# Which engine subtracts the low parts of an input projection's weights: GpSimd or VectorE

## The chip, the cores and the metric

The kernel runs on one core of a Trainium2 chip. The core has five engines that each work through a row of instructions of their own, in order: TensorE (PE: matrix products and transposes), VectorE (DVE), ScalarE (ACT), GpSimd (POOL) and SyncE (SP, which issues the DMAs). An instruction starts when the one ahead of it on its engine is through and the semaphores that it waits for are set. The metric is the time of one execution on the device, in microseconds (us).

## The reference

One layer of a hybrid block over a sequence of S = 1024 rows of D = 1024 numbers, all float32:

```python
u = rms_norm(h, norm_gain)
proj = u @ w_in                      # -> z_ssd, xbc, dt_raw, q, k, v, z_attn
xbc = silu(causal_depthwise_conv(xbc, conv_w, conv_b))        # 4 taps
dt = softplus(dt_raw + dt_bias);  a = -exp(a_log)
y = ssd_chunked(xs, dt, a, B, C) + xs * d_skip                # chunks of 128 rows
y_ssd = gated_group_rms_norm(y, z_ssd, ssd_norm_gain)
attn = diff_attention(q, k, v, lam, slopes)   # two softmaxes a head, one minus lam times the other
y_attn = rms_norm(attn, subln_gain) * (1 - lambda_init) * silu(z_attn)
h = h + concat([y_ssd, y_attn]) @ w_out
out = rms_norm(h, final_norm_gain)
```

## The kernel before

The two big projections are made on PE in a split form. Each operand is held as a high part, rounded to the type fp32r, and a low part, which is the operand minus the high part; a product is then three matmuls: high by high, high by low and low by high. For the input, `uh` and `ul` are made once at the start (L188 and L189, in two halves of 512 rows). The weights come in blocks of 128 columns: SP's queue loads `raw` (two buffers), ACT rounds it to `hi` (L199), and the low part `lo` is `raw - hi` (L200). `load_w` does this for two blocks at a time, into two buffers each of `hi` and `lo` (the tags whi and wlo). It is called 25 times: for B and C (bc, names of tiles lo_bc0 and so on), the conv inputs (xs), the gate of the SSD part (z), the queries and keys of a head (qk), the values of two heads (v) and their gate (za). The very first block (z0 with dt) isn't made by `load_w` but by a loop of its own, L333 to L343, with its subtraction on GpSimd at L342.

The program's stages are: the normalization of x (square sums on ACT, L173 and L175 the reciprocal root on GpSimd, L183 the scaling on DVE, L187 eight rounds of transposes on PE); the first block (L352 to L357, eight tiles of 128 rows, in two PSUM banks named mm); two groups g of the SSD part; and eight attention heads, whose projections are woven among the heads' own work, and the output projection. In a group, L281 and L282 (ACT) take a conv input from PSUM, L287 (DVE) adds three taps, L291 (ACT) is the tanh, L292 (DVE) finishes it; L374 and L376 make the masked product of B and C, L432 transposes, L457 and L463 are the group's other work on GpSimd. In attention, L557 makes a block of scores (PE), L563 adds the distance and takes the row maximum (DVE), L573 scales it, L581 is the exponential (ACT), L590, L591 and L594 weigh the two maps (DVE), L602 transposes them (PE), L605 copies them (ACT), and L609 multiplies by the values (PE). L507 and L508 take the queries out of their mm bank, L518 and L519 the keys; the bank is free for PE's next projection (L208 to L210 by columns, L217 to L219 by rows) after the DVE one of the two. L614 takes an attention output from PSUM. Some low parts of the output projection's weights are subtracted on GpSimd (L694, first half) and some on DVE (L694, second half, named wp_lo).

The order in which each engine gets its instructions isn't the order of the code: a scheduler arranges them by a simulated timeline of all engines, so that a change of one instruction's engine also moves others.

Of the kernel before, what the change touches and what calls it, by code (L numbers as in the profile page):

```python
# [8 lines left out]
F32 = mybir.dt.float32  # L9
# [3 lines left out]
ALU = mybir.AluOpType  # L13
# [25 lines left out]
def kernel(  # L39
# [11 lines left out]
    V, A, G, T = nc.vector, nc.scalar, nc.gpsimd, nc.tensor  # L51
# [8 lines left out]
    def big_tile(tag, bufs, shape, dt=F32, name=None):  # L60
        return big.tile(shape, dt, tag=tag, bufs=bufs, name=name or tag)
# [7 lines left out]
    def tG(shape, dt=F32, name="tG"):  # L69
        return big_tile("G", 13, shape, dt, name)  # L70
# [47 lines left out]
    def load_raw(blocks, name):  # L118
        raws = []
        for n, b in enumerate(blocks):  # L120
            raw = tRaw(f"raw_{name}{n}")
            dma(raw, w_blocks[b])
            raws.append(raw)
        return raws
# [69 lines left out]
    def load_w(b0, b1, name, raws=None):  # L194
        hi = big_tile("whi", 2, [P, ND, 2 * P], F32R, f"hi_{name}")
        lo = big_tile("wlo", 2, [P, ND, 2 * P], F32R, f"lo_{name}")
        for n, raw in enumerate(raws or load_raw((b0, b1), name)):
            cut = slice(n * P, (n + 1) * P)
            A.activation(hi[:, :, cut], raw, AF.Copy)  # L199
            G.tensor_tensor(lo[:, :, cut], raw, hi[:, :, cut].bitcast(F32), ALU.subtract)  # L200
        return hi, lo

    def proj_ch(w, n, half, ps):
# [130 lines left out]
    for d0, d1 in D3:  # L334
        hi, lo = (tG([P, d1 - d0, NZ], F32R, f"wz_{n}{d0}") for n in ("hi", "lo"))
        for n, raw in enumerate(raw_z0 + [wdt_raw]):
            cut = slice(n * P, min(NZ, (n + 1) * P))
# [22 lines left out]
    def ssd_group(g):  # L360
        hs = slice(8 * g, 8 * g + 8)
        w = load_w(B_XBC + 8 + g, B_XBC + 10 + g, f"bc{g}", raw_bc0 if g == 0 else None)
        if g == 0:
            bT, cT = conv_first(w)
# [18 lines left out]
        for k in range(2):  # L383
            w = load_w(B_XBC + 4 * g + 2 * k, B_XBC + 4 * g + 2 * k + 1, f"xs{g}{k}")
            for n in range(2):
                xsT.append(conv(w, n, 4 * g + 2 * k + n))
        if g == 0:
            z0 = z_first
        else:
            zw = load_w(B_Z + 4 * g, B_Z + 4 * g + 1, f"z{g}0")  # L390
            z0 = [proj_gate_half(zw, half, f"z{g}0{half}") for half in range(2)]
# [475 lines left out]
```

## Time and profile before

| | us |
|---|---|
| median of 3 runs | 1061.67 (1061.25 to 1062.02) |
| the profiled execution | 1060.02 |
| its span, first to last instruction | 1058.3 |
| PE busy | 1026.2 |
| DVE busy | 579.2 |
| ACT busy | 504.9 |
| POOL busy | 237.1 |

In the rows of the profile, L12 is line 12 of the program. A row of a timeline gives the start, the duration, the engine, the line, the operation, what is written and read with its shape, how many instructions are joined in the row, and in brackets how long the engine was idle ahead of it and what it waited for. A row of a group gives the total, the mean in ns and, behind the second bar, the idle time ahead of the group's instructions. A row of PE's waits gives the waiting and the awaited instruction, the total in us, the number of times and the longest. A row of a window gives the stretch, its length, the busy time and count of PE, of its weight loads (PEld), DVE, ACT and POOL, and then the clock granted to PE (1 is full), the share of DMA and GB/s. In a timeline the ends of an instruction and the start of the next overlap by some hundredths.

### The profile page before, as it was taken

The page shows a single profiled execution, that of the slowest core. Times are in us where ns is not written, and L with a number is a line of the kernel's source. Part 1 is how long each engine was busy: PE and PEld are TensorE (multiplying, and loading weights), DVE is VectorE, ACT ScalarE, POOL GpSimd, SP SyncE. Part 2 cuts the span into 40 slices and gives each one's busy share as a digit, 9 for nine tenths or more (in the row PEclk, how much of TensorE's full clock was granted, in tenths as well). Part 3 has the DMA queues.
Part 4 walks back from the last instruction along what each step waited for, and adds up shares of the span by engine and source line. Part 5 has one row for each costly group of instructions (what it writes and reads, how often), then busy time and mean ns, then how long its engine had stood idle before and what let it go on. Part 6 is the DMA issues. An engine that isn't in the chain of part 4 may idle for free.

```text
span 1058.3 us, 16243 instructions
## 1 busy us (share of the span) xinstructions
PE 1026.2 (97%) x6334; PEld 910.3 (86%) x6334; DVE 579.2 (55%) x1235; ACT 504.9 (48%) x1137; POOL 237.1 (22%) x191
## 2 busy tenths in 40 slices
PE   5999999989999999999999999999999998999997
PEld 5988887878987999889998899988998987788887
DVE  5546578665567264473563744627547587462221
ACT  8244367834456554453453554534646556341110
POOL 7212226422343312210222022111220340010000
PEclk9999999999999999999999999999999999999999
DMA  7111124221224311312103221033211533354211
GB/s 288 41 62 41 60 71 130 80 60 60 81 62 138 101 41 41 80 40 71 41 15 95 61 61 61 11 80 80 62 55 31 155 115 127 135 158 140 80 45 40
DMA packets 52085, 84.54 MB, mean 80 GB/s; under 512 B 3932, under 2 KB 30633, under 8 KB 52009
## 3 DMA queue, kind: packets, MB, share of 16 engines
q1 hardware_dynamic: 52008, 83.51, 25.5%
q8 instruction: 50, 0.82, 0.3%
q14 instruction: 27, 0.21, 0.1%
HBM read 62.45 MB, written 12.65 MB: 71 GB/s over the span
## 4 chain that ended last, share of the span: by engine, by line
PE 88%; DVE 5%; ACT 3%; DMA 2%; issue 2%; SPq 0%; POOLq 0%; DVEq 0%; ACTq 0%
PE mm L208 9%; PE mm L209 9%; PE mm L210 9%; PE mm L217 8%; PE mm L218 8%; PE mm L219 8%; PE o L609 6%; PE S L557 5%; PE mm L709 5%; PE mm L710 5%; PE mm L711 5%; PE tp L602 3%; PE S L439 3%; PE S L448 1%; PE S L452 1%
## 5 line engine op out<-in xcount | busy, mean ns | idle before, releaser
L563 DVE CUSTOM_DVE_ANT_0 s<-S,dist 128x256 f32<-128x256 f32 (+7 forms) x128 | 95.1, 754 | 99.8 <-PE S L557 94.5
L581 ACT ACTIVATE s<-s,small 128x256 f32<-128x256 f32 (+7 forms) x128 | 98.8, 772 | 89.4 <-DVE small L573 88.5
L208 PE MATMUL mm<-uh,hi_qk 128*128 128x512 f32 x256 | 101.4, 396 | 0.3 <-DVE k L519 0.3
L210 PE MATMUL mm<-uh,lo_qk 128*128 128x512 f32 x256 | 101.5, 396 | 0.0
L209 PE MATMUL mm<-ul,hi_qk 128*128 128x512 f32 x256 | 100.7, 393 | 0.0
L557 PE MATMUL S<-k,q 128*128 128x512 f32 (+2 forms) x384 | 92.8, 356 | 2.3 <-DVE small L563 2.3
L605 ACT ACTIVATE wT<-tp 128x512 f32<-128x512 f32 (+2 forms) x96 | 46.5, 485 | 82.9 <-PE tp L602 82.4
L609 PE MATMUL o<-v,wT 128*128 128x128 f32 x576 | 80.3, 276 | 0.0
L609 PEld LDWEIGHTS o<-v,wT 128*128 128x128 f32 x576 | 75.1, 193 | 2.4
L557 PEld LDWEIGHTS S<-k,q 128*128 128x128 f32 x384 | 65.1, 189 | 12.4 <-DVE small L563 4.2
L287 DVE SCALAR_TENSOR_TENSOR ca<-cr,cwb,ca 128x1023 f32<-128x1023 f32 (+2 forms) x36 | 56.8, 1578 | 33.3 <-ACT ca L282 32.5
L217 PE MATMUL mm<-hi_v,uh 128*128 128x256 f32 x256 | 73.6, 288 | 1.1 <-DVE q L508 0.9
L219 PE MATMUL mm<-hi_v,ul 128*128 128x256 f32 x256 | 73.4, 287 | 0.0
L218 PE MATMUL mm<-lo_v,uh 128*128 128x256 f32 x256 | 73.4, 287 | 0.0
L219 PE MATMUL mm<-hi_za,ul 128*128 128x256 f32 x256 | 73.0, 285 | 0.0
L217 PE MATMUL mm<-hi_za,uh 128*128 128x256 f32 x256 | 73.0, 285 | 0.0
L218 PE MATMUL mm<-lo_za,uh 128*128 128x256 f32 x256 | 73.0, 285 | 0.0
L200 POOL TENSOR_TENSOR lo_qk<-raw_qk,hi_qk 128x1024 fp32r<-128x1024 f32 x16 | 38.5, 2427 | 127.8 <-ACT hi_qk L199 127.8
L217 PE MATMUL mm<-hi_z,uh 128*128 128x256 f32 x192 | 56.1, 292 | 0.3 <-DVE z L322 0.3
L210 PEld LDWEIGHTS mm<-uh,lo_qk 128*128 128x128 f32 x256 | 48.1, 188 | 9.5 <-issue 0.2
L208 PEld LDWEIGHTS mm<-uh,hi_qk 128*128 128x128 f32 x256 | 48.2, 188 | 9.1 <-DVE k L519 0.6
L209 PEld LDWEIGHTS mm<-ul,hi_qk 128*128 128x128 f32 x256 | 48.2, 188 | 9.0
(217 smaller groups left out, 2762.7 us busy)
## 6 DMA issues: line engine op xcount, KB each, us to landing
m<-acs_d SPq DMA_DIRECT2D x16, 512.0 KB, 3.8
raw_qk<-in_w_blocks_dram SPq DMA_DIRECT2D x16, 512.0 KB, 3.6
q<-q SPq DMA_DIRECT2D x32, 256.0 KB, 3.0
rwo<-in_w_out_dram SPq DMA_DIRECT2D x16, 512.0 KB, 3.5
rt<-tt_d SPq DMA_DIRECT2D x27, 256.0 KB, 3.7
x<-in_x_dram SPq DMA_DIRECT2D x8, 512.0 KB, 6.2
raw_z<-in_w_blocks_dram SPq DMA_DIRECT2D x8, 512.0 KB, 3.5
raw_xs<-in_w_blocks_dram SPq DMA_DIRECT2D x8, 512.0 KB, 3.7
```

What stands on the lines that cost most here:

```text
L208: T.matmul(ps, hi[:, d, cut], uh[half][:, d, :], start=(d == 0), stop=False)
L209: T.matmul(ps, hi[:, d, cut], ul[half][:, d, :], start=False, stop=False)
L210: T.matmul(ps, lo[:, d, cut], uh[half][:, d, :], start=False, stop=(d == ND - 1))
L217: T.matmul(ps, uh[half][:, d, cut], hi[:, d, :], start=(d == 0), stop=False)
L218: T.matmul(ps, uh[half][:, d, cut], lo[:, d, :], start=False, stop=False)
L219: T.matmul(ps, ul[half][:, d, cut], hi[:, d, :], start=False, stop=(d == ND - 1))
L287: V.scalar_tensor_tensor(acc[:, k:S], raw[:, 0 : S - k], cwb[:, c : c + 1], acc[:, k:S], op0=ALU.mult, op1=ALU.add)
L557: T.matmul(os[m], qs[half][m][:, part, qcut], ks[kh][:, m, :width], start=(part == 0), stop=(part == 1))
L563: V.tensor_tensor_reduce(out=s[:, :n], in0=ps[:, :n], in1=dist[:, S - n : S], op0=ALU.add, op1=ALU.max, scale=1.0, scalar=-3.0e38, accum_o ...
L581: A.activation(s[:, :n], s[:, :n], AF.Exp, bias=nb[:, m : m + 1], scale=slope, accum_out=sums[:, m, ii : ii + 1],)
L609: T.matmul(po[:, qcut], wT[:, kb, :], vs[kb // 4][:, kb % 4, vcut], start=(kb == 0), stop=(kb == i))
L709: T.matmul(ps, th[:, k, :], hi, start=(kt == first), stop=False)
```

## The change

In `load_w`, the subtraction of L200 goes from GpSimd's row to VectorE's. It is 50 instructions of 128 x 1024 elements (16 for qk, 8 each for xs, v and za, 6 for z and 4 for bc). GpSimd keeps L342, the reciprocal roots, L457, L463, the first half of L694 and a few others: its row goes from 191 instructions to 141.

```diff
@@ -197,7 +197,7 @@
         for n, raw in enumerate(raws or load_raw((b0, b1), name)):
             cut = slice(n * P, (n + 1) * P)
             A.activation(hi[:, :, cut], raw, AF.Copy)
-            G.tensor_tensor(lo[:, :, cut], raw, hi[:, :, cut].bitcast(F32), ALU.subtract)
+            V.tensor_tensor(lo[:, :, cut], raw, hi[:, :, cut].bitcast(F32), ALU.subtract)
         return hi, lo
```

The scheduler puts the 50 instructions into DVE's row, and shifts others: most by a few places. Three places follow. First the start of DVE's row, before: the last L189 of the first half of the rows, then L488 (lambda), the gates of the first two tiles (L356 and L357, which free a bank), and the scalings of x4 and x5.

```order
L189 SCALAR_TENSOR_TENSOR ul0_138<-o_207,ng_126,uh0_136 128x512
L189 SCALAR_TENSOR_TENSOR ul0_138<-S1_214,ng_126,uh0_136 128x512
L189 SCALAR_TENSOR_TENSOR ul0_138<-S1_221,ng_126,uh0_136 128x512
L488 TENSOR_TENSOR lams_118<-lams_118 128x128
L490 TENSOR_REDUCE ls_3092<-lams_118 128x2
L356 SCALAR_TENSOR_TENSOR z000_352<-z000_352,mm_353 128x256
L357 TENSOR_TENSOR dtmp_327<-mm_353,vecs_116 128x16
L356 SCALAR_TENSOR_TENSOR z000_352<-z000_352,mm_381 128x256
L357 TENSOR_TENSOR dtmp_327<-mm_381,vecs_116 128x16
```

The same stretch of DVE's row now.

```order
L189 SCALAR_TENSOR_TENSOR ul0_138<-o_207,ng_126,uh0_136 128x512
L200 TENSOR_TENSOR lo_bc0_613<-raw_bc00_108,hi_bc0_612 128x8x128
L189 SCALAR_TENSOR_TENSOR ul0_138<-S1_214,ng_126,uh0_136 128x512
L200 TENSOR_TENSOR lo_bc0_613<-raw_bc01_109,hi_bc0_612 128x8x128
L189 SCALAR_TENSOR_TENSOR ul0_138<-S1_221,ng_126,uh0_136 128x512
L183 TENSOR_SCALAR x4_91<-x4_91,r_x4_233 128x1024
L488 TENSOR_TENSOR lams_118<-lams_118 128x128
L183 TENSOR_SCALAR x5_92<-x5_92,r_x5_241 128x1024
L490 TENSOR_REDUCE ls_3092<-lams_118 128x2
L183 TENSOR_SCALAR x6_93<-x6_93,r_x6_249 128x1024
L229 TENSOR_SCALAR nega_319<-nega_319 128x16
L356 SCALAR_TENSOR_TENSOR z000_352<-z000_352,mm_353 128x256
```

Two lo_bc0 stand among the L189; x4 to x6 are scaled ahead of the first gate, where they stood behind the second. PE's row, before, ahead of the third tile (mm_409), which needs the bank that the first gate frees:

```order
L354 MATMUL mm_353<-wz_hi6_344,ul0_138 128x272
L354 MATMUL mm_381<-wz_hi6_344,ul0_138 128x272
L352 MATMUL mm_409<-wz_hi0_328,uh0_136 128x272
L353 MATMUL mm_409<-wz_lo0_329,uh0_136 128x272
L354 MATMUL mm_409<-wz_hi0_328,ul0_138 128x272
```

and PE's row now at the same tile:

```order
L187 MATMUL S1_274<-ident_82,x6_93 128x128
L187 MATMUL S1_281<-ident_82,x6_93 128x128
L187 MATMUL tp_288<-ident_82,x6_93 128x128
L187 MATMUL o_295<-ident_82,x6_93 128x128
L352 MATMUL mm_409<-wz_hi0_328,uh0_136 128x272
```

The transposes of x4, x5 and x6, six each, stand ahead of the third tile now; the last four of those 18 rows are the ones shown.

The second place is DVE's row in group 1, around the first conv input cv4 that follows B and C; before:

```order
L376 TENSOR_TENSOR cbm1_1872<-o_1874,tri_316 128x512
L292 SCALAR_TENSOR_TENSOR cv4_1966<-cr4_1907,ca4_1908 128x1024
L429 TENSOR_TENSOR m10_2391<-m10_2391,cbm1_1872 128x1024
L376 TENSOR_TENSOR cbm1_1872<-o_1886,tri_316 128x512
L287 SCALAR_TENSOR_TENSOR ca5_1970<-cr5_1969,cwb_125,ca5_1970 128x1023
```

and now:

```order
L376 TENSOR_TENSOR cbm1_1872<-o_1874,tri_316 128x512
L292 SCALAR_TENSOR_TENSOR cv4_1966<-cr4_1907,ca4_1908 128x1024
L200 TENSOR_TENSOR lo_z10_2166<-raw_z100_2167,hi_z10_2165 128x8x128
L429 TENSOR_TENSOR m10_2391<-m10_2391,cbm1_1872 128x1024
L200 TENSOR_TENSOR lo_z10_2166<-raw_z101_2169,hi_z10_2165 128x8x128
L376 TENSOR_TENSOR cbm1_1872<-o_1886,tri_316 128x512
L287 SCALAR_TENSOR_TENSOR ca5_1970<-cr5_1969,cwb_125,ca5_1970 128x1023
```

The two lo_z10 stand behind cv4's L292, on either side of L429. (In group 0 the two lo_z01 stand in the same way in one piece, directly ahead of the three taps of ca1.)

The third place is DVE's row in the last block but one of head 3 (s36), where the queries of head 4 (q411) leave their bank; before:

```order
L563 ISA s361_5712,small36_5697<-S_5699,dist_3086 128x896
L563 ISA small36_5697 128x1
L573 TENSOR_SCALAR small36_5697<-small36_5697 128x1 x2
L614 TENSOR_SCALAR oc30_5600<-o_5468 128x512
L508 SCALAR_TENSOR_TENSOR q411_5912<-mm_5886,q411_5912 64x512
L590 RECIPROCAL small36_5697<-sums31_5620 128x1
```

and now:

```order
L563 ISA s361_5712,small36_5697<-S_5699,dist_3086 128x896
L563 ISA small36_5697 128x1
L200 TENSOR_TENSOR lo_za2_6481<-raw_za20_6482,hi_za2_6480 128x8x128
L573 TENSOR_SCALAR small36_5697<-small36_5697 128x1
L200 TENSOR_TENSOR lo_za2_6481<-raw_za21_6484,hi_za2_6480 128x8x128
L508 SCALAR_TENSOR_TENSOR q411_5912<-mm_5886,q411_5912 64x512
L519 TENSOR_TENSOR k41_5944<-mm_5919,k41_5944 64x512
```

Both lo_za2 now stand between the row maxima (L563) and L508. The same holds for lo_za3 at the queries q611 of head 6; lo_za1, lo_v1 and lo_v3 also stand closely ahead of an L508 or L519.

## The prediction

> **What bounds the kernel now.** I read the busy shares and the chain first, then the waits of TensorE (PE), then the timeline of the places where those waits fall.
>
> ```profile
> PE 1026.2 (97%) x6334; PEld 910.3 (86%) x6334; DVE 579.2 (55%) x1235; ACT 504.9 (48%) x1137; POOL 237.1 (22%) x191
> PE 88%; DVE 5%; ACT 3%; DMA 2%; issue 2%; SPq 0%; POOLq 0%; DVEq 0%; ACTq 0%
> PE S L187 <- DVE x L183: 7.3, 1, 7.3
> PE tp L602 <- ACT wT L605: 3.3, 3, 2.1
> PE mm L352 <- DVE dtmp L357: 3.1, 2, 2.4
> PE S L557 <- DVE small L563: 2.3, 3, 1.6
> PE tp L432 <- DVE cv L292: 2.2, 2, 1.6
> PE mm L353 <- POOL wz_lo L342: 0.6, 1, 0.6
> ```
>
> PE is busy 97% of 1058.3 us: 32 us of idle are all that any other engine's work can give back, 7.3 of them before the first transpose. The view of PE's waits has sixteen rows; fifteen name VectorE (DVE) or ScalarE (ACT), and GpSimd (POOL) stands in one, for L342, which stays. So no wait on the 50 subtractions of L200 is there to be removed, and their time on POOL is worth nothing in itself. What they cost is indirect: while POOL runs, some DVE instructions take longer, and those do end PE's waits.
>
> ```profile
> L694 DVE TENSOR_TENSOR wp_lo<-rwo,wp_hi 128x1024 fp32r<-128x1024 f32 x8 | 9.7, 1223 | 2.7 <-ACT wT L605 1.7 <-ACT wp_hi L693 0.6 <-PE mm L710 0.4
> L200 POOL TENSOR_TENSOR lo_qk<-raw_qk,hi_qk 128x1024 fp32r<-128x1024 f32 x16 | 38.5, 2427 | 127.8 <-ACT hi_qk L199 127.8
> L287 DVE SCALAR_TENSOR_TENSOR ca<-cr,cwb,ca 128x1023 f32<-128x1023 f32 (+2 forms) x36 | 56.8, 1578 | 33.3 <-ACT ca L282 32.5
> 214.00 1.28 DVE L287 SCALAR_TENSOR_TENSOR ca<-cr,cwb,ca 128x1021 f32<-128x1021 f32 x1
> ```
>
> **The price.** L694 is the same subtraction on DVE, same shape and types: 1.223 us against 2.427 on POOL. Fifty of them add 50 x 1.223 = 61.2 us to DVE (579 to 640 of 1058, 60%), so DVE does not become the bound; on a lone instruction the chain gets 1.2 us shorter. A conv tap L287 with POOL silent takes 1.28 (row at 214.00), the mean of the 36 is 1.578: 36 x 0.3 = 11 us of DVE time lie in that one group and come back. What counts is where these lie on PE's path.
>
> [...]
>
> **Place A, the start (20 to 31 us).**
>
> ```profile
> 18.05 4.71 POOL L200 TENSOR_TENSOR lo_bc<-raw_bc,hi_bc 128x1024 fp32r<-128x1024 f32 x2
> 22.85 0.73 POOL L173 TENSOR_SCALAR m_x<-ssx 128x1 f32<-128x1 f32 x3
> 20.87 2.05 DVE L488 TENSOR_TENSOR lams<-lams 128x128 f32<-128x128 f32 x1 [1.30 <-DMA lams<-in_vectors_dram]
> 23.80 0.36 PE L352 MATMUL mm<-wz_hi,uh 128*128 128x272 f32 x1 [2.40 <-DVE dtmp L357]
> 18.82 0.75 DVE L189 SCALAR_TENSOR_TENSOR ul<-S,ng,uh 128x512 fp32r<-128x512 f32 x1 [0.78 <-ACT uh L188]
> 20.98 0.41 PE L354 MATMUL mm<-wz_hi,ul 128*128 128x272 f32 x2
> 24.00:29.00 5.00, 5.00 (x29) 5.00 (x29) 4.02 (x7) 1.95 (x3) 4.83 (x6) 0.66 0.01 3
> 220.47 1.05 PE L374 MATMUL o<-cv,cv 128*128 128x128 f32 x8
> ```
>
> POOL's two lo_bc run 18.05 to 22.76. Behind them wait DVE's L488 (2.05 us, ended with POOL) and, behind L488 in DVE's row, the L357 that frees the mm bank for L352: PE idles 2.40. They also hold POOL's own rsqrt steps for x4 to x7 until 22.85. After the idle the granted clock is 0.66 over 24 to 29 (next to last three columns), with PE busy all 5 us: up to 5 x 0.34 = 1.7 us lost. In the new order POOL goes straight to the rsqrt steps, and PE has 18 transposes (x4 to x6) ahead of that L352, so the hole is filled: 18 x 0.13 (L374, 1.05 for 8) = 2.3 us of work out of the way. L352 itself has to wait for three scalings more on DVE, some 0.6 to 1.1 us past 23.80: +0.8. The clock, with no idle of that length: -1.7. Against it, both lo_bc stand on DVE ahead of the last two L189: the last, ended 19.57 before, comes 1.2 to 2.4 later, 20.8 to 22.0, where PE's L354 wants it at 20.98: 0 to 1.0, +0.5 taken. Sum -2.7; ends -4.1 (clock and hole whole) and -1.0 (the clock drops all the same).
>
> **Place B, 98 to 108 us.**
>
> ```profile
> 96.09 5.74 POOL L200 TENSOR_TENSOR lo_z<-raw_z,hi_z 128x1024 fp32r<-128x1024 f32 x2 [19.77 <-ACT hi_z L199]
> 98.15 6.08 DVE L287 SCALAR_TENSOR_TENSOR ca<-cr,cwb,ca 128x1023 f32<-128x1023 f32 x3 [3.70 <-ACT ca L282]
> 106.69 0.33 PE L432 MATMUL tp<-ident,cv 128*128 128x128 f32 x1 [0.58 <-DVE cv L292]
> 107.50 0.50 PE L208 MATMUL mm<-uh,hi_xs 128*128 128x512 f32 x1 [0.48 <-ACT ca L282]
> 105.00:108.00 3.00, 1.94 (x8) 1.17 (x8) 1.23 (x1) 1.71 (x4) 0.00 (x0) 1.00 0.00 0
> ```
>
> Three taps take 6.08 instead of 3 x 1.28 = 3.84, 2.2 us too long, and the L292 at their end ends two idles of PE, 0.58 + 0.48. In the new order both lo_z01 stand ahead of the taps, in the 3.70 us in which DVE waits for L282: the second ends about 0.3 after 98.15, and the chain is 1.9 us earlier. -1.1; ends -1.6 (PE is busy just 1.94 of 3 us here) and 0.
>
> **Place C, 220 to 230 us.**
>
> ```profile
> 221.58 5.66 POOL L200 TENSOR_TENSOR lo_z<-raw_z,hi_z 128x1024 fp32r<-128x1024 f32 x2 [12.17 <-ACT hi_z L199]
> 222.17 2.84 DVE L292 SCALAR_TENSOR_TENSOR cv<-cr,ca 128x1024 f32<-128x1024 f32 x1
> 105.41 1.23 DVE L292 SCALAR_TENSOR_TENSOR cv<-cr,ca 128x1024 f32<-128x1024 f32 x1 [1.19 <-ACT cr L291]
> 222.31 1.16 PE L374 MATMUL o<-cv,cv 128*128 128x128 f32 x8 [0.78 <-DVE cbm L376]
> 225.07 0.33 PE L432 MATMUL tp<-ident,cv 128*128 128x128 f32 x1 [1.60 <-DVE cv L292]
> 225.88 0.66 PE L208 MATMUL mm<-uh,hi_xs 128*128 128x512 f32 x1 [0.48 <-ACT ca L282]
> 226.00:230.00 4.00, 4.00 (x11) 3.17 (x12) 4.00 (x3) 0.50 (x1) 1.24 (x1) 0.57 0.62 195
> ```
>
> L292 takes 2.84 beside POOL and 1.23 without (row at 105.41): 1.61 us, which is the 1.60 that PE idles. Then 4 us at a clock of 0.57: 4 x 0.43 = 1.7 lost. In the new order L292 comes ahead of both lo_z10, so it runs alone: -1.6. B's idles of about 1.1 us left the clock at 1.00, and about as much idle stays here, so by that nearest row the drop goes too: -3.3; ends -3.3 and -1.6.
>
> **Places D, attention: where it costs.** DVE is in order, and there L508 and L519 free the mm banks for PE.
>
> ```profile
> 478.51 0.39 PE L602 MATMUL tp<-ident,s 128*128 128x128 f32 x1 [2.12 <-ACT wT L605]
> 479.00:483.00 4.00, 4.00 (x24) 4.00 (x24) 3.90 (x8) 1.23 (x6) 0.00 (x0) 0.62 0.83 239
> 611.21 0.27 DVE L573 TENSOR_SCALAR small<-small 128x1 f32<-128x1 f32 x2
> 613.93 0.39 PE L217 MATMUL mm<-hi_v,uh 128*128 128x256 f32 x1
> 746.21 0.15 DVE L573 TENSOR_SCALAR small<-small 128x1 f32<-128x1 f32 x1
> 748.92 0.38 PE L217 MATMUL mm<-hi_v,uh 128*128 128x256 f32 x1 [0.94 <-DVE q L508]
> 713.56 2.40 DVE L591 SCALAR_TENSOR_TENSOR small<-sums,small,neglam 128x1 f32<-128x1 f32 x1
> ```
>
> For lo_za2 and lo_za3 both subtractions now stand between the row maxima (ended by 611.3 and 746.3) and L508. 611.3 + 1.22 + 0.15 (L573) + 1.22 + 0.7 (L508) = 614.6, where L217 started at 613.93: +0.7; the same sum at 746.3 gives 749.6 against 748.92: +0.7. For lo_v1 and lo_v3 two subtractions come before an L519, 1 us later than now, while the L591 held up by POOL (2.40 at 713.56) gets short again: +0.5 each, since PE shows no idle there now (ends 0 and 1.2). lo_za1: the 2.12 of idle goes, because 24 matmuls of L217 to L219 now stand ahead of that second group of transposes, but they wait for an L508 behind both subtractions, by the same addition some 1.6 us: -0.5, with the slow clock (4 x 0.38 = 1.5) kept; ends -2.0 and +0.5. Sum of D +1.9; ends -0.5 and +4.5.
>
> The rest of the 50 lie in gaps of DVE in which it waits for PE or ACT: cost 0, cover those gaps. Orders of PE and DVE also shift behind 783 us, where no L200 is left; nothing there gets a price, only a bound, the longest late idle of the kind L557 <- L563, 1.6 us to either side. No DMA is added; raw tiles come free 1.2 us sooner per pair.
>
> **Sum.** -2.7 - 1.1 - 3.3 + 1.9 = -5.2. The profiled execution took 1060.02 (span 1058.3 and 1.7 around it), 1.65 below the median of 1061.67; the same step on the median gives 1056.5.
>
> **Rivals.** First, given back, within 0.2% (2.1 us, about what this measurement can tell from no change): PE's slow clock of A and C comes all the same. Then A is -1.0, C -1.6, B -1.1, and D +1.9: -1.8, 1059.9. For it: the drop at 226 followed three short idles, of 0.8, 1.6 and 0.5 us, none of them long. Against it: B. [...]
>
> Second, slower: DVE's queue in attention. The five pairs of D (v1, za1, za2, v3, za3) hold L508 and L519 by up to 2 x 1.22 = 2.45 each, 12.2 in all. At half of it on PE's path, 6.1, and one drop of 1.5 added, 7.6 - 3.7 (A to C with the drops kept) = +3.9: 1065.6. It decides from 3.7 / 5 = 0.75 us a place on; the two that I could add up come to 0.7. Against it: PE has other work in its row at v1 and v3, and POOL's hold on DVE goes.
>
> Third, larger: D free by cover and all clocks kept: -2.7 - 1.1 - 3.3 - 0.5 = -7.6, 1054.1; with A whole 1052.7.
>
> That the change does not do what it says is excluded by the order: all 50 stand on DVE.
>
> **Numbers.** Forecast with its larger neighbour 0.62 (0.47 and 0.15), given back 0.22, slower 0.16. The likeliest time is 1056.5. The given-back case reaches from 1059.6 to 1063.8 and most of it lies low; the range goes from 1052.7 to 1062.3, which leaves out the slower case and a few hundredths at each end. Faster 0.62, same 0.22, slower 0.16.
>
> **What would show it.** A right: no PE idle near 21.4 to 23.8, PEclk near 1 over 24 to 29, L488 short. B and C: taps at 1.28, L292 at 1.23, no idle at L432, clock 1 at 226. D right: L217 at the za places waits for L508 about 0.7 longer. Wrong: idle over 2 us ahead of L217 or L208 with clock drops behind it in 440 to 750, or PE slowed after 24 and 226 without idle.

## The result, and the profile after

The change makes the kernel 10.8 us faster: 1050.63 us (1049.18 to 1050.97, 4 runs) against 1061.46 (1060.86 to 1062.02) beside it, ratio 0.9909, 95% interval 0.9892 to 0.9926. A second measurement, the experiment after_again, gave 1049.15 against 1059.50, 0.9900 (0.9885 to 0.9915). The forecast was faster, 1056.5 in a range of 1052.7 to 1062.3: the side was right, the size is double.

The page of the changed kernel, first the busy times, then the first rows of PE's waits.

```profile
PE 1021.0 (97%) x6334; PEld 906.2 (87%) x6334; DVE 586.8 (56%) x1285; ACT 505.7 (48%) x1137; POOL 114.2 (11%) x141
PE S L187 <- DVE x L183: 8.7, 4, 7.2
PE o L609 <- ACT wT L605: 2.5, 4, 1.1
PE mm L709 <- ACT th L656: 1.6, 2, 1.0
PE tp L602 <- ACT wT L605: 1.2, 2, 0.7
PE mm L217 <- DVE q L508: 0.9, 2, 0.5
```

POOL's time falls by 123 us. DVE takes 50 instructions more and is busy only 7.6 us longer. L432 <- L292 (2.2 before) is gone, L352 <- L357 is down from 3.1 to 0.5, L602 <- L605 from 3.3 to 1.2; L609 <- L605, which before doesn't have, comes in with 2.5. The groups of DVE show where its time came from, first two rows of before, then rows of the changed kernel:

```profile
L402 DVE TENSOR_TENSOR y<-y,z 128x256 f32<-128x256 f32 x32 | 23.3, 758 | 1.2 <-POOL y L463 0.8
L591 DVE SCALAR_TENSOR_TENSOR small<-sums,small,neglam 128x1 f32<-128x1 f32 x64 | 28.0, 438 | 1.6
L200 DVE TENSOR_TENSOR lo_qk<-raw_qk,hi_qk 128x1024 fp32r<-128x1024 f32 x16 | 19.1, 1221 | 2.6 <-ACT hi_qk L199 2.6
L287 DVE SCALAR_TENSOR_TENSOR ca<-cr,cwb,ca 128x1023 f32<-128x1023 f32 (+2 forms) x36 | 46.2, 1282 | 12.9 <-ACT ca L282 12.1
L402 DVE TENSOR_TENSOR y<-y,z 128x256 f32<-128x256 f32 x32 | 14.8, 494 | 2.3 <-POOL y L463 2.1
L591 DVE SCALAR_TENSOR_TENSOR small<-sums,small,neglam 128x1 f32<-128x1 f32 x64 | 14.2, 222 | 1.6
```

A subtraction takes the forecast 1.22 us. The taps L287 take 1.282 each (1.578 before), L402 0.494 (0.758), and L591, which works on one column, 0.222 (0.438).

The places A, B and C of the prediction, in the timelines and windows of the changed kernel:

```profile
23.09 0.66 PE L187 MATMUL S<-ident,x 128*128 128x128 f32 x4 [0.54 <-DVE x L183]
24.00:29.00 5.00, 4.44 (x37) 4.44 (x38) 4.57 (x12) 2.01 (x4) 1.10 (x2) 1.00 0.09 16
93.67 2.36 DVE L200 TENSOR_TENSOR lo_z<-raw_z,hi_z 128x1024 fp32r<-128x1024 f32 x2 [1.55 <-ACT hi_z L199]
95.95 3.92 DVE L287 SCALAR_TENSOR_TENSOR ca<-cr,cwb,ca 128x1023 f32<-128x1023 f32 x3
218.17 1.22 DVE L292 SCALAR_TENSOR_TENSOR cv<-cr,ca 128x1024 f32<-128x1024 f32 x1
220.25 0.50 PE L208 MATMUL mm<-uh,hi_xs 128*128 128x512 f32 x1 [0.48 <-ACT ca L282]
222.00:226.00 4.00, 4.00 (x19) 3.34 (x18) 3.93 (x5) 0.00 (x0) 0.00 (x0) 1.00 0.75 244
```

At A the one idle of 2.40 has become three, of 0.38, 0.54 (the row shown) and 0.59, between the transposes, and the clock (third column from the end) is 1.00 where it was 0.66. At B three taps take 3.92 (6.08 before). At C L292 takes 1.22 (2.84 before), PE doesn't wait for it, and the clock is 1.00 (0.57 before). And the places D, in attention:

```profile
465.35 1.16 PE L609 MATMUL o<-v,wT 128*128 128x128 f32 x8 [1.08 <-ACT wT L605]
469.60 0.39 PE L217 MATMUL mm<-hi_v,uh 128*128 128x256 f32 x1 [0.36 <-DVE q L508]
472.00:476.00 4.00, 4.00 (x37) 4.00 (x36) 3.87 (x8) 2.05 (x8) 0.00 (x0) 1.00 0.17 34
603.77 0.39 PE L217 MATMUL mm<-hi_v,uh 128*128 128x256 f32 x1 [0.55 <-DVE q L508]
737.09 1.16 PE L609 MATMUL o<-v,wT 128*128 128x128 f32 x8 [0.54 <-ACT wT L605]
```

The first three rows are lo_za1: its one idle of 2.12 has become 1.08 and 0.36, and the clock is 1.00. At lo_za2 PE waits 0.55 for an L508, at lo_za3 0.54 for an L605.

To put all kernels on one scale, I gave each of PE's 6334 instructions the interval that it usually takes in the trace of before (0.227 us for a matmul of 512 columns, 0.120 for 256, 0.109 to 0.112 for most of 128), added them up in order (1011 us in all), and compared the times at which two kernels have the same sum behind them. The first column is the time at which before has it; the others give how much later (minus: earlier) the kernel has it. The names of the experiments follow below.

| before at | after | ssd_on_dve | att_on_dve | six_on_dve | dve_twice | pool_read | pool_write | ghost_read |
|---|---|---|---|---|---|---|---|---|
| 35 | -2.1 | -1.3 | -0.3 | -2.0 | +2.3 | -1.4 | -1.7 | +5.0 |
| 97 | -2.3 | -1.5 | -0.3 | -2.1 | +1.2 | -1.6 | -1.9 | +4.0 |
| 118 | -3.9 | -3.1 | -0.3 | -3.7 | +1.2 | +2.1 | -3.5 | +2.7 |
| 220 | -4.0 | -3.2 | -0.3 | -3.6 | +2.5 | +2.0 | -3.6 | +13.8 |
| 245 | -7.3 | -6.4 | -0.6 | -6.8 | +4.4 | +1.9 | -6.8 | +11.3 |
| 266 | -7.9 | -7.1 | -0.6 | -6.8 | +4.5 | +5.6 | -7.5 | +10.6 |
| 406 | -8.0 | -7.1 | -0.7 | -6.8 | +5.2 | +5.5 | -7.6 | +10.5 |
| 490 | -10.4 | -8.5 | -3.1 | -6.8 | +5.2 | +3.1 | -10.0 | +8.1 |
| 813 | -10.0 | -6.7 | -2.6 | -5.0 | +10.9 | +3.5 | -9.6 | +8.5 |
| 897 | -11.3 | -5.9 | -4.4 | -3.8 | +10.9 | +2.2 | -11.2 | +6.9 |
| 941 | -11.3 | +0.4 | -3.2 | +1.2 | +12.1 | +2.2 | -11.2 | +6.9 |

So by the two traces the change gains 2.3 at A, 1.5 at B, 3.3 at C, 0.7 at 261, 2 in attention and 1.3 near the end.

### The profile page after: what moved, and what is told of

Its sections match the earlier page's. It is cut to its first block, busy times and chain, and to the rows that moved or that the text cites. A ratio compares the mean times of both kernels' runs of the same rounds, so it can differ in the third digit from the quotient of the medians.

```text
span 1047.4 us, 16245 instructions
## 1 busy us (share of the span) xinstructions
PE 1021.0 (97%) x6334; PEld 906.2 (87%) x6334; DVE 586.8 (56%) x1285; ACT 505.7 (48%) x1137; POOL 114.2 (11%) x141
## 4 chain that ended last, share of the span: by engine, by line
PE 89%; issue 3%; ACT 3%; DVE 2%; DMA 1%; POOL 1%; POOLq 0%; DVEq 0%; SPq 0%; ACTq 0%
PE mm L208 9%; PE mm L209 9%; PE mm L210 9%; PE mm L217 8%; PE mm L218 8%; PE mm L219 8%; PE mm L709 6%; PE mm L710 6%; PE mm L711 6%; PE o L609 5%; PE S L557 5%; PE S L439 3%; PE tp L602 3%; PE S L448 1%; PE S L452 1%
## 5 line engine op out<-in xcount | busy, mean ns | idle before, releaser
L563 DVE CUSTOM_DVE_ANT_0 s<-S,dist 128x256 f32<-128x256 f32 (+7 forms) x128 | 94.5, 755 | 111.2 <-PE S L557 103.9
L581 ACT ACTIVATE s<-s,small 128x256 f32<-128x256 f32 (+7 forms) x128 | 98.5, 770 | 72.1 <-DVE small L573 71.5
L557 PE MATMUL S<-k,q 128*128 128x512 f32 (+2 forms) x384 | 90.6, 355 | 0.5 <-DVE small L563 0.5
L605 ACT ACTIVATE wT<-tp 128x512 f32<-128x512 f32 (+2 forms) x96 | 46.6, 485 | 77.7 <-PE tp L602 77.2
L609 PE MATMUL o<-v,wT 128*128 128x128 f32 x576 | 79.9, 275 | 2.5 <-ACT wT L605 2.5
L609 PEld LDWEIGHTS o<-v,wT 128*128 128x128 f32 x576 | 74.3, 191 | 6.6 <-ACT wT L605 3.7
L594 DVE SCALAR_TENSOR_TENSOR s<-s,small,s 128x128 f32<-128x128 f32 (+3 forms) x64 | 54.2, 848 | 1.6
L219 PE MATMUL mm<-hi_z,ul 128*128 128x256 f32 x192 | 55.0, 287 | 0.0
```

What stands on the lines that cost most here:

```text
L219: T.matmul(ps, ul[half][:, d, cut], hi[:, d, :], start=False, stop=(d == ND - 1))
L557: T.matmul(os[m], qs[half][m][:, part, qcut], ks[kh][:, m, :width], start=(part == 0), stop=(part == 1))
L563: V.tensor_tensor_reduce(out=s[:, :n], in0=ps[:, :n], in1=dist[:, S - n : S], op0=ALU.add, op1=ALU.max, scale=1.0, scalar=-3.0e38, accum_o ...
L581: A.activation(s[:, :n], s[:, :n], AF.Exp, bias=nb[:, m : m + 1], scale=slope, accum_out=sums[:, m, ii : ii + 1],)
L609: T.matmul(po[:, qcut], wT[:, kb, :], vs[kb // 4][:, kb % 4, vcut], start=(kb == 0), stop=(kb == i))
```

## The experiments

**Which instructions carry it.** Three kernels move only a part of the 50.

```diff
 # ssd_on_dve
-            G.tensor_tensor(lo[:, :, cut], raw, ...)
+            (V if name[:2] in ("bc", "xs") or (name[0] == "z" and name[1] != "a") else G).tensor_tensor(lo[:, :, cut], raw, ...)
 # att_on_dve: V and G exchanged
 # six_on_dve
+            (V if name in ("bc0", "z01", "z10") else G).tensor_tensor(lo[:, :, cut], raw, ...)
```

> Only the 18 subtractions of the SSD stage (bc, xs, z) on VectorE, the 32 of attention (qk, v, za) on GpSimd as before. Theory (VectorE instructions with two SBUF inputs are no longer held up by GpSimd at three places of PE's path): by 380 us PE's work is 8.0 us ahead of before, as in the changed kernel (2.3 at the start, 1.5 at 105, 3.3 at 225, 0.7 at 261, the rest small), and attention adds what its own order makes of it, within 2.5 us either way: 1053.5, 1051 to 1056. Rival (the gain comes from the whole program's new order, not from these places): the first 380 us are ahead by less than 5, total above 1057.

Measured: 1059.97, ratio 1.0000 (0.9988 to 1.0011): no change. The first part came as the theory had it, 7.1 earlier at 266. Then some 2 us were lost between 510 and 530. The new order has put a pair of GpSimd's subtractions beside other VectorE instructions there:

```profile
506.10 4.74 POOL L200 TENSOR_TENSOR lo_qk<-raw_qk,hi_qk 128x1024 fp32r<-128x1024 f32 x2
506.16 2.35 DVE L632 TENSOR_TENSOR r_o<-r_o,keep 128x4 f32<-128x4 f32 x1 [1.48 <-POOL r_o L175]
508.55 3.23 DVE L641 SCALAR_TENSOR_TENSOR t<-oc,r_o,za 128x128 f32<-128x128 f32 x4
512.17 0.61 PE L557 MATMUL S<-k,q 128*128 128x384 f32 x2 [1.64 <-DVE small L563]
```

L632 takes 2.35 where it has a mean of 0.159 in before, four L641 take 3.23 where four take 1.14 at 918.11 of the same trace, and PE idles 1.64 for the row maximum behind them: the mechanism of the change, here at a place of PE's path where before has no idle. Another 6.3 were lost between 897 and 941, a stretch in which no L200 is left. There this kernel's timeline and windows show:

```profile
919.16 2.35 DVE L694 TENSOR_TENSOR wp_lo<-rwo,wp_hi 128x1024 fp32r<-128x1024 f32 x2
921.44 0.15 DVE L754 TENSOR_SCALAR ssf<-ssf 128x1 f32<-128x1 f32 x1
918.61 1.03 PE L647 MATMUL tp<-ident,t 128*128 128x128 f32 x4 [0.79 <-DVE t L641]
921.58 0.80 PE L710 MATMUL mm<-wp_lo,th 128*128 128x512 f32 x1 [1.94 <-DVE ssf L754]
922.00:926.00 4.00, 4.00 (x10) 3.08 (x10) 0.18 (x1) 0.00 (x0) 0.00 (x0) 0.50 0.00 0
```

PE idles 0.79 for an L641 and 1.94 for L754, ahead of which two L694 stand in DVE's row, and then runs 4 us at half the clock. The scheduler has arranged the end of the program anew.

> Only the 32 subtractions of attention (qk, v, za) on VectorE, the 18 of the SSD stage on GpSimd as before. Its order in attention is nearly that of the changed kernel. Theory from the two traces: attention and the late part gain 3.3 us (the idle of 2.12 and the slow clock at 478 go, and 1.3 in 860 to 885): 1058.2, 1057 to 1059.5. Rival, the prediction's step D: subtractions ahead of L508 and L519 cost 1.9 in attention: 1063.4, slower than before.

Measured: 1056.58, 0.9975 (0.9965 to 0.9985), 3.2 us earlier at the end of the trace. The theory's 3.3 for the stage is about met, and the prediction's step D is refuted: the 32 subtractions of attention, with nearly the order that they have in the changed kernel, make the program faster, not 1.9 slower. Of the 2.4 gained between 406 and 490, though, ssd_on_dve has 1.4 with none of these 32 moved: PE idles the same 2.12 there as in before, but no slow clock follows (1.00 from 470 to 485, where before has 0.62 from 479 to 483).

> Only six subtractions on VectorE: lo_bc0, lo_z01 and lo_z10, those of the places A, B and C; 44 stay on GpSimd. Theory: these six carry 7.1 us of the change (2.3, 1.5 and 3.3): PE's work is 7.1 ahead by 240 us, total 1054.4, within 2.5 for the order of the rest. Rival (many small releases over all 50 make the gain): less than 3 us, above 1058.

Measured: 1062.58, 1.0026 (1.0017 to 1.0036), slower than before. At 245 it is 6.8 earlier, so the six do carry nearly all of the gain up to there (7.3). It then loses 1.9 at 510 to 530 and 5.0 between 897 and 941, like ssd_on_dve (L632 at 2.35 and PE's idle of 1.64 again, and the same wait of L710, 1.9 us). My total was wrong for both kernels: I had allowed the rest of the order 2.5 us, and it took 6.5 and 8.

**Is it GpSimd's reading, or the order?** Four kernels leave the 50 on VectorE. In pool_read and pool_write GpSimd gets work of no use, behind VectorE's subtraction, at six tiles (z01, z10, z11); the order of PE, DVE and ACT is the changed kernel's, row for row.

```diff
 # pool_read
+            name in ("z01", "z10", "z11") and G.tensor_tensor(raw, raw, hi[:, :, cut].bitcast(F32), ALU.subtract)
 # pool_write
+            [G.memset(raw, 0.0) for _ in range(2) if name in ("z01", "z10", "z11")]
 # ghost_read: at the 18 tiles of the SSD stage, into a scratch tile
+            [G.tensor_tensor(junk, raw[:, d, :], hi[:, d, cut].bitcast(F32), ALU.subtract) for d in range(ND) if ...]
```

> The changed kernel once more, beside the kernels that are compared with it: 1050.6, 0.9909 of before. If part of its gain is a slow clock of TensorE that comes in some executions and not in others, its fast runs spread with the granted clock as those of before do (28 runs of before: 1056.8 at a clock of 0.999, 1060.2 at 0.994), and the gain at equal clock is 7 to 8 us, the rest being fewer slow stretches.

Measured: 1049.15, 0.9900 (0.9885 to 0.9915), its four runs at a clock of 0.998 to 0.999. The 28 runs of before that the experiments above shared had, in the mean, 1056.8 at 0.999 (4 runs), 1059.5 at 0.996 (9), 1060.2 at 0.994 (13) and 1061.2 at 0.992 (2); the one run of before at 0.999 beside after_again had 1057.0. At the same clock of 0.999 the gain is so 1056.8 - 1049.2 = 7.6 us; the other 3 are slow stretches of PE that the changed kernel mostly avoids. In the trace of before, which has a clock of 0.994, the three slow stretches (A, C and 478) cost more, some 1.4, 1.6 and 1.7 us by the longer intervals of their matmuls; no trace of a run of before at 0.999 is there to compare. Below, where the changed kernel didn't run beside another, it is taken at 0.9900 of before.

> The changed kernel; GpSimd also computes the six subtractions of z01, z10 and z11 into the raw tile, behind VectorE's, read by nobody. The order of TensorE, VectorE and ScalarE is word for word that of the changed kernel. Theory (GpSimd's reads hold up VectorE instructions with two SBUF inputs): taps of ca1 at place B, or the L429 at place C, take 2 to 4 us longer, and PE's idle at 105 comes back: 1 to 4 us slower than the changed kernel, 1051.6 to 1054.6. Rival (order or an earlier low part makes the gain): no change, 1050.6 within 0.8.

Measured: 1062.92, 1.0031 (1.0020 to 1.0043): 13.8 us slower than the changed kernel beside it, from six instructions that nobody waits for. Place B in the timelines of this kernel, the row of PE's waits and a window:

```profile
95.67 6.63 POOL L200 TENSOR_TENSOR raw_z<-raw_z,hi_z 128x1024 f32<-128x1024 f32 x2 [69.75 <-DVE lo_z L200]
96.64 8.06 DVE L287 SCALAR_TENSOR_TENSOR ca<-cr,cwb,ca 128x1023 f32<-128x1023 f32 x3
107.17 0.33 PE L432 MATMUL tp<-ident,cv 128*128 128x128 f32 x1 [2.69 <-DVE cv L292]
PE tp L432 <- DVE cv L292: 7.0, 3, 2.7
109.00:113.00 4.00, 4.00 (x12) 3.13 (x11) 3.81 (x3) 0.08 (x1) 0.00 (x0) 0.57 0.00 0
```

The three taps, 3.92 in the changed kernel, take 8.06, and PE waits 2.69 for what follows them; the pair on POOL is stretched too, 6.63 for two. The last row is the window behind that idle, at a clock of 0.57; the 4 us from 266 have 0.57 as well. Against the changed kernel, the table has 5.3 us lost at B, 3.2 between 220 and 245 (the L292 of place C runs in 1.22 here; a subtraction and a tap behind it are held up, and PE idles 2.19 at 239.64) and 4.4 at 261. I had the direction and less than a third of the size. These 12.9 us are more than the 5.5 that the change gains at the same places, so this run shows the cause and not its price in before: GpSimd's pair at B starts 1 us ahead of the taps here and 2 us ahead of them there.

> As pool_read, with the same six waits, but GpSimd writes zeros to the raw tile twice instead of reading. The order of the three engines is again that of the changed kernel. If reading is what collides: within 0.8 us of the changed kernel. If any work on GpSimd, or the raw tile held longer, is what costs: as slow as pool_read.

Measured: 1048.96, 0.9901 (0.9886 to 0.9917): as the changed kernel. This row is its 12 writes, 1.9 us for a pair:

```profile
L200 POOL MEMSET raw_z<- x12: 953/956/960, 95.3 to 248.0; 128x1024 f32 x12
```

So at these six tiles neither a busy GpSimd, nor its waits, nor a raw tile held 1.9 us longer (2.4 to 3.4 in pool_read) costs anything that can be measured (1048.96 against 1049.15 for after_again); its reading does (1062.92, and 8.06 against 3.92 for the taps). In the trace of before, the VectorE instructions named here that grew beside a pair of GpSimd's read two operands from SBUF: the taps (6.08 for three), L292 (2.84), L591 (2.40) and L183, where one of the two is a column (2.85 at 27.37, median 0.754). Those with one operand from SBUF kept their time inside the pair that runs from 609.69 to 614.42: L563 with 1.09, two L573 with 0.27, L508 with 0.69.

> The changed kernel; for the 18 tiles of the SSD stage GpSimd also subtracts in 8 pieces of 128 columns each, as soon as the high part is there, into a scratch tile read by nobody. The order of the other engines is nearly that of the changed kernel (92 rows of PE differ). Theory: at A, B and C VectorE instructions are held up again, and so are GpSimd's roots at the start: 3 to 7 us slower than the changed kernel, 1053.6 to 1057.6. Rival: within 1 us.

Measured: 1066.68, 1.0066 (1.0051 to 1.0081), 17.5 slower than the changed kernel: the theory's direction, at more than twice its size. Many short reads of about 0.46 us stand between GpSimd's own steps and delay them as well (PE's waits for L183, which follow the roots, are 11.6 in sum against 8.7): in the table it is 7 us behind the changed kernel at 35 and 18 at 220.

The same was done in attention: GpSimd subtracts into raw, behind VectorE, at the 32 tiles of qk, v and za.

> The changed kernel; for the 32 tiles of attention (qk, v, za) GpSimd also subtracts into the raw tile, behind VectorE's, read by nobody; the order of the other engines is nearly that of the changed kernel (78 rows of PE differ). Theory: in attention too GpSimd's reads hold up VectorE (L591 2.4 instead of 0.22 us, L594 and L200 longer), and the 3 us that attention and the end gained come back: 1052 to 1057. Rival (the gain in attention is order alone): 1049.2 within 1.

Measured: 1058.45, 0.9978 (0.9969 to 0.9986), some 8 us slower than the changed kernel. From its groups and its waits of PE:

```profile
L591 DVE SCALAR_TENSOR_TENSOR small<-sums,small,neglam 128x1 f32<-128x1 f32 x64 | 30.0, 468 | 1.6
L594 DVE SCALAR_TENSOR_TENSOR s<-s,small,s 128x128 f32<-128x128 f32 (+3 forms) x64 | 64.4, 1007 | 1.6
PE tp L602 <- DVE s L594: 3.3, 3, 2.6
PE mm L217 <- DVE q L508: 2.3, 2, 1.7
```

L591 is back near its old mean (0.222 in the changed kernel), L594 is at 1.007 (0.848), and PE waits for L594 and for L508. GpSimd's reads cost in attention too. They start later than in before, so this is no measure of what they cost there.

**Is the price on VectorE hidden?** Each subtraction is issued twice in a row.

```diff
             V.tensor_tensor(lo[:, :, cut], raw, hi[:, :, cut].bitcast(F32), ALU.subtract)
+            V.tensor_tensor(lo[:, :, cut], raw, hi[:, :, cut].bitcast(F32), ALU.subtract)
```

> The changed kernel, with each of the 50 subtractions issued twice in a row on VectorE, the second writing the same numbers again: 61 us more on VectorE, nothing on GpSimd. If a subtraction's 1.22 us on VectorE is hidden beside other work (DVE busy 587 of 1047), the time stays within 2.5 us of the changed kernel's 1050.6. Rival, the prediction's step D: they lie on PE's path ahead of L508 and L519 at five places, each then 1.2 to 2.4 later: 6 to 12 us slower, 1057 to 1063.

Measured: 1072.80, 1.0124 (1.0106 to 1.0143): some 23 us slower than the changed kernel for 61 us of work, twice the rival's upper figure. Three of its waits of PE that the changed kernel lacks or has shorter:

```profile
PE o L374 <- ACT tT L412: 2.9, 1, 2.9
PE mm L217 <- DVE q L508: 2.2, 2, 1.7
PE mm L352 <- DVE dtmp L357: 1.5, 1, 1.5
```

The order changed much here, so the 23 us are not the queue alone. But the mechanism of step D exists: at 2.4 us a block, VectorE's row ends PE's waits more often; at 1.2 it does so for 0.36 and 0.55 us in attention.

**Can more be moved?** Three further steps from GpSimd to VectorE, each on top of the change.

```diff
 # scan_on_dve: L457 and L463;  all_wo: L694;  first_on_dve: L342
-                    G.tensor_tensor(...)
+                    V.tensor_tensor(...)
```

> The changed kernel, with the 12 multiplications of L457 and the 14 additions of L463 on VectorE too, which leaves GpSimd almost nothing to read in the SSD stage. Theory: L402, L429 and others lose their last collisions, 13 us of VectorE time that lies mostly off PE's path, which has one idle of 0.78 there: 1049.2 within 1.2. Rival (VectorE's own row gets too long): 2 us slower or more.

Measured: 1049.68, 0.9901 (0.9888 to 0.9915): as the changed kernel. L402 falls to 0.420 us and PE's path does not notice.

> The changed kernel, with the eight subtractions of L694 that GpSimd keeps (first half of the output weights) on VectorE too. Theory: the late part (820 to 900 us), where 6 us of PE idle are left, changes by order more than by collisions: 1049.2, 1047 to 1053. Rival (GpSimd's last long reads cost there as in the SSD stage): 2 us faster or more, below 1047.2.

Measured: 1058.24, 0.9982 (0.9973 to 0.9991): some 8.5 us slower than the changed kernel, lost between 813 and 941, where the changed kernel has about 4 us of idle (820 to 900) and not the 6 that the theory names.

```profile
PE o L609 <- ACT wT L605: 4.2, 4, 1.9
PE mm L710 <- DVE ssf L754: 2.1, 1, 2.1
```

It is the wait of L710 that ssd_on_dve had, with the slow clock behind it (0.52 from 920 to 925). Neither theory nor rival had it: both looked at the late idles that were there, not at one that a new order makes.

> The changed kernel, with L342 (the first block's nine subtractions) on VectorE too. VectorE is the busier engine there (x scaled, ul), GpSimd has the roots: PE's first tile waits for wz_lo 0.6 us now. Theory: within 1 us of 1049.2, since what L342 frees on GpSimd lets the roots of x4 to x7 start earlier but lengthens VectorE's row ahead of ul. Rival (the row of VectorE ahead of ul decides): 1 to 3 us slower.

Measured: 1055.23, 0.9951 (0.9937 to 0.9964): some 5 us slower than the changed kernel. The rival had the place; the size is nearly twice its upper figure; PE now waits for ul, as the prediction feared for the two lo_bc0, and for the first gate:

```profile
PE mm L352 <- DVE dtmp L357: 2.1, 1, 2.1
PE mm L354 <- DVE ul L189: 1.9, 1, 1.9
```

None of the three beats the changed kernel.

## Why the prediction was wrong in size

- The mechanism was right for the SSD stage: no wait on L200 was removed, and at B, at C and at 261 the time came from VectorE instructions that GpSimd's reads no longer hold up. pool_read and pool_write show with an unchanged order that such reads cost at B, behind C and at 261. At A it is argued only. L488 falls from 2.05 to 0.28, but GpSimd's roots also start earlier, at 19.84 instead of 22.85, because no lo_bc stands ahead of them in its row, and 18 transposes fill the hole; no run separates the three.
- A, B and C were right in size: -2.7, -1.1 and -3.3 forecast, -2.3, -1.5 and -3.3 measured, 7.1 in sum both times. That the sums are equal is luck. At A two misses work against each other: the last L189 ended at 20.76, in time for PE, where +0.5 was forecast, and PE idled 1.51 for the three scalings, where +0.8 was. The rise of the clock at A and C came as forecast, 0.66 and 0.57 to 1.00.
- **The step that failed is D, +1.9 forecast, -2.0 measured** (from 406 to 813 in the table): 3.9 of the 5.6 us by which the forecast falls short; the late part has 1.3 and 261 has 0.7. The largest part of D is lo_za1: -0.5 forecast, with 1.6 us of idle and the slow clock kept; in its place came 1.08 and 0.36 of idle and a clock of 1.00, and the table has -2.4 from 406 to 490. For lo_za2 and lo_za3 I had +1.4 by adding durations behind L563; PE's idle there went from 0.37 to 0.26 + 0.55 and from 0.94 to 0.26 + 0.54, +0.3 in sum. The two L519 of v1 and v3 were put at +1.0 and cost nothing; L591's 2.4 us in the same place went, as I had noted without giving it a price. The two ends of D add up to -0.6 and +4.3, not to -0.5 and +4.5, which changes nothing.
- What lo_za1 gained comes from no collision. In before, the 2.12 of idle ends with an L605 of ACT, whose row is busy without a gap from 475.33 on (L581, L617, L507, L518):

```profile
477.38 0.59 ACT L518 ACTIVATE k<-mm 64x512 fp32r<-64x512 f32 x1
477.88 0.58 ACT L605 ACTIVATE wT<-tp 128x512 f32<-128x512 f32 x1
```

  The L591 that GpSimd holds up there (1.01 us) isn't in that chain. In the changed kernel that L605 comes directly behind an L581, and 24 matmuls stand ahead of PE's transposes. So the shorter idle is order, and the rest, some 1.5 us, is the slow clock that didn't follow; ssd_on_dve lost that slow clock without the order, and six_on_dve, with 2.1 of idle at an L602 and no gain in the table from 406 to 490, seems to have kept it.
- DVE's busy time was forecast at 640 and is 586.8. I had counted the 11 us that come back in the group of L287 alone. Summed over its instructions, DVE gets 61.3 us of subtractions and grows by 14.5, so 47 come back: L591 has 13.8, L287 10.6, L402 8.5, L429 3.2 and L292 2.3. (The busy time grows by 7.6 only, because ends that overlap the next start count once.) This isn't what step D missed: from 406 to 813 DVE's busy time rises all the same, from 215.6 to 230.0.
- The term "nothing gets a price behind 783, 1.6 to either side" was too narrow: the changed kernel gains 1.3 there, but ssd_on_dve and six_on_dve lose 6 to 7 behind 813, where no L200 is left, by the order and a slow clock behind it (0.50 from 922 to 926 in ssd_on_dve, 0.81 and 0.85 in the two 5 us from 920 in six_on_dve), and all_wo 8.5 with eight subtractions of that stage moved. The changed kernel's 1.3 is order too: the idle of before at 878.60, 1.59, comes when GpSimd has been silent for 12 us. The 0.7 at 261 I had put at 0.
- The rival "given back" was wrong on the clock in this trace, and the rival "slower" lies between the changed kernel and dve_twice.

Open stays what each of the three parts of A is worth, and what GpSimd's reads cost in attention in before: pool_read_att shows that later ones cost there, and no run has before's reads with the new order.

## What to carry to other kernels

Work that nobody waits for can still be what costs (six such instructions cost 13.8 us in pool_read): look for instructions of one shape whose duration varies (L292 here, 1.23 or 2.84), and for what GpSimd reads beside the long ones, before you put its work at nothing. When a scheduler orders the program, cost a moved instruction by its stage, and expect several us of either sign from the stages behind it, where the instruction does not even occur (here -1.3 to +7.1 behind 813); a pair of kernels in which GpSimd's work is added back, once reading and once only writing, with the order held, tells the two apart (here 1062.92 and 1048.96).

## What the runs showed that I had not expected

- One column's worth of work (L591, 0.22 us) takes up to 2.42 us beside a GpSimd subtraction, and GpSimd's own 2.4 us grow to as much as 3.4 (lo_z of before) when VectorE is at it.
- An idle of PE of the same length costs the clock or doesn't. At the same transposes of lo_za1, with 2.12 us of idle each time, before fell to 0.62 in the 4 us from 479 and ssd_on_dve stayed at 1.00:

```profile
471.42 0.33 PE L602 MATMUL tp<-ident,s 128*128 128x128 f32 x1 [2.12 <-ACT wT L605]
470.00:475.00 5.00, 3.58 (x29) 3.46 (x30) 4.87 (x7) 3.08 (x11) 0.59 (x1) 1.00 0.92 283
475.00:480.00 5.00, 5.00 (x45) 5.00 (x44) 3.53 (x16) 3.24 (x6) 1.20 (x2) 1.00 0.11 25
```

The clock also fell behind an idle of 2.40 us (A of before, to 0.66), behind 0.79 and 1.94 (ssd_on_dve, 0.50), behind 2.69 and 0.48 (B of pool_read, 0.57) and, at C of before, behind 0.78, 1.60 and 0.48 (0.57). What decides whether it falls, no run shows.
